# Eight orders of the products of a weight unit, taken in turn, with the order of all stream products fixed

## Chip, cores and metric

The kernel runs on one core of one Trainium2 chip. The metric is the device time of one execution in microseconds (us), lower is better. TensorE is called PE, VectorE DVE, ScalarE ACT; DMAs of the weights are issued from SyncE (SP).

## What is computed

The reference is a trunk of four residual layers on x of 256 tokens and 2048 channels: a state-space mixer, a gated conv feed-forward, a gated short convolution, and a second gated conv feed-forward, with a norm ahead of each and one at the end. Nearly all the work lies in products with large weight matrices. Cut to that:

```python
for i in range(DEPTH):                      # DEPTH = 2
    h = rms_norm(x, mix_norm_w[i])
    if i % 2 == 0:
        x = x + ssd_mixer(h, ...)           # u @ w_in (2048 x 10304), state-space part, y @ w_out (4096 x 2048)
    else:
        x = x + short_conv_mixer(h, ...)    # u @ w_in (2048 x 6144), conv, gate, @ w_out (2048 x 2048)
    h = rms_norm(x, ffn_norm_w[i])
    x = x + conv_ffn(h, ...)                # u @ w_up (2048 x 11264), conv, silu(g) * v, @ w_down (5632 x 2048)
return rms_norm(x, final_norm_w)
```

All values are float32.

## The kernel before

Every weight matrix is read once, in **units** of 256 rows (two slices k of 128 rows) by 512 columns (four column blocks t of 128). `load_unit` (lines 249 to 262) brings a unit in by a DMA from SP, ACT rounds it to a high part `wh` (line 260, the CAST), and DVE takes the rest as a low part `wl` (line 261). Four pairs of buffers `wh`, `wl` exist (`WB = 4`), so the cast of a unit waits until PE has used up the unit four places earlier. The activations lie in pairs of 128-channel slices, each split in a high and a low part that stand side by side in a tile `hl`.

`stream` (line 274) multiplies a run of units, mostly 8 of them, with the activations. For each of the eight (t, k) of a unit it issues a **wide** product, the high weights times high and low activations together, 512 columns (line 296), and a **narrow** one, the low weights times the high activations, 256 columns (line 297): 16 products. Where `one` is set (the streams for B, C and xs of the state-space mixer) the wide product is issued as two of 256 columns (lines 293 and 294), 24 products to a unit. All products of a (column block t) add up in one bank of PSUM; a stream has two tiles of two banks each, `pts[0]` for t = 0, 1 and `pts[1]` for t = 2, 3, out of a pool `psm` of three such tiles. So `pts[0]` of a stream takes the tile that is free, and `pts[1]` the tile that was `pts[0]` of the stream before, as soon as that has been read out. The reading out is done by `evac`: a copy by ACT (line 306) and a sum by DVE (line 308), or two sums by DVE (lines 634 and 636) in `residual_stream`, or one product with the norm's row (line 314) where `one` is set.

There are 84 streams of wide and narrow products with 696 units, 12 streams with `one` and 96 units, and the last down projection, in which tokens lie on partitions: 88 units of 12 products of 512 columns each (lines 794 to 796). Other matrix products (transposes, norm sums, the state-space part: lines 176, 183, 449, 566, 585, 593 and others) write to two further banks, `aux`.

The order in which PE takes its instructions is not that of the program text: the kernel is built with a scheduler that lays out each engine's queue by a model of the times. In the program's order a unit's products go t = 0, k = 0 wide, narrow; k = 1 wide, narrow; t = 1, and so on. The scheduler leaves this order in places. At the start of most streams it puts the products into `pts[0]` of the first units ahead of those into `pts[1]`, so that a narrow product of one tile is put off, or two wide ones follow each other; and at the end of the state-space mixer it interleaves products of two streams. There `ssd_gate` of the last group (line 603, under `tc.high_priority()`) prepares the last two pairs of activations of the first `residual_stream` of the output projection: its products with the six earlier units can run before that, those with the last two units cannot.

Of the kernel before, what the change touches and what calls it, by code (L numbers as in the profile page):

```python
# [13 lines left out]
PSUM = bass.MemoryType.PSUM  # L14
DRAM = bass.MemoryType.DRAM

P = 128
T = 256
# [14 lines left out]
KU = 2  # L33
COLS = 512
# [5 lines left out]
def trunk_kernel(ctx, tc, a, out):  # L40
    nc = tc.nc
    mm = nc.tensor.matmul
# [14 lines left out]
    psa = ctx.enter_context(tc.tile_pool(name="psa", bufs=2, space=PSUM))  # L57

    n_id = [0]

    def uid(s):
        n_id[0] += 1
# [5 lines left out]
    def aux():  # L68
        return psa.tile([P, 512], F32, tag="aux", name=uid("aux"))

# [1 line left out]
    mixer = ExitStack()  # L72
    bcpool = mixer.enter_context(tc.tile_pool(name="bcpool", bufs=4))
    xspool = mixer.enter_context(tc.tile_pool(name="xspool", bufs=3))
    start = ExitStack()
# [9 lines left out]
                in_=a["x"][0, c * P : (c + 1) * P, q * 512 : (q + 1) * 512],  # L85
            )

# [1 line left out]
    ident = cpool.tile([P, P], F32, tag="ident", name="ident")  # L89
    make_identity(nc, ident)  # L90
    ones = cpool.tile([P, P], F32, tag="ones", name="ones")
    nc.vector.memset(ones, 1.0)
    mask3 = cpool.tile([P, 3, P], F32, tag="mask3", name="mask3")
    # Nothing reads these products: they keep the tensor engine clocked up until x arrives.
    warm = psa.tile([P, 512], F32, tag="aux", name="warm")
    for _ in range(9):
        mm(warm[:, 0:P], ones, ones, start=True, stop=True)
# [3 lines left out]
    nc.vector.tensor_copy(mask3[:, 1, :], ones)  # L101
    nc.vector.tensor_copy(mask3[:, 2, :], triu)

# [1 line left out]
    rows = [  # L105
        ("mix", a["mix_norm_w"].rearrange("l (k p) -> (l k) p", p=P)),
        ("ffn", a["ffn_norm_w"].rearrange("l (k p) -> (l k) p", p=P)),
# [16 lines left out]
    for name, r in rows:  # L124
        base[name] = at
        lo = 0
        while lo < r.shape[0]:
            i, off = divmod(at, P)
# [20 lines left out]
    load_x(0)  # L149
    load_params(0)  # L150

# [1 line left out]
    def rsqrt(v, n):  # L153
        """v**-0.5 for v > 0, [P, n], from an integer seed by Newton's method."""
        r = small.tile([P, n], F32, tag="rs_r", name=uid("rs_r"))
        t = small.tile([P, n], F32, tag="rs_t", name=uid("rs_t"))
        sh = small.tile([P, n], I32, tag="rs_i", name=uid("rs_i"))
        ts(out=sh, in0=v.bitcast(I32), scalar1=1, scalar2=None, op0=ALU.logical_shift_right)
        ts(
            out=r.bitcast(I32), in0=sh, scalar1=-1.0, scalar2=float(0x5F3759DF),  # L160
            op0=ALU.mult, op1=ALU.add,
        )
        for _ in range(3):
            stt(out=t, in0=r, scalar=-0.5, in1=v, op0=ALU.mult, op1=ALU.mult)
            tt(out=t, in0=t, in1=r, op=ALU.mult)
            stt(out=r, in0=t, scalar=1.5, in1=r, op0=ALU.add, op1=ALU.mult)
        return r

    def bcast_tok(r):
        """r [tokens, 2] -> PSUM [P, 256], the same row on every partition."""  # L170
        dg = small.tile([P, 2, P], F32, tag="dg", name=uid("dg"))
        ps = aux()
        for c in range(2):
            ts(out=dg[:, c, :], in0=ident, scalar1=r[:, c : c + 1], scalar2=None, op0=ALU.mult)
        for c in range(2):
            mm(ps[:, c * P : (c + 1) * P], ones, dg[:, c, :], start=True, stop=True)  # L176
        return ps[:, :T]

    def tok_sum(acc):
        """Column sums of acc [P, 256] -> PSUM [tokens, 2]."""  # L180
        ps = aux()
        for c in range(2):
            mm(ps[:, c : c + 1], acc[:, c * P : (c + 1) * P], ones[:, 0:1], start=True, stop=True)
        return ps[:, 0:2]
# [11 lines left out]
        return (pool or hlpool).tile([P, 2, 2 * T], F32R, tag="hl", name=uid("hl"))  # L196

    def split_pair(hl, src, wname=None, k0=0):
        """hl[:, j] = [high | low] parts of src[:, j] (times a per-channel weight)."""
        if wname is None:  # L200
            nc.scalar.copy(hl[:, :, 0:T], src)
            tt(out=hl[:, :, T : 2 * T], in0=src, in1=hl[:, :, 0:T].bitcast(F32), op=ALU.subtract)
            return
        for j in range(2):
            w = pcol(wname, k0 + j)
            act(hl[:, j, 0:T], src[:, j, :], AF.Copy, scale=w)
            stt(  # L207
                out=hl[:, j, T : 2 * T], in0=src[:, j, :], scalar=w,
                in1=hl[:, j, 0:T].bitcast(F32), op0=ALU.mult, op1=ALU.subtract,
            )  # L210

# [1 line left out]
    s_in, s_out = a["ssd_w_in"][0], a["ssd_w_out"][0]  # L213
    c_in, c_out = a["sc_w_in"][0], a["sc_w_out"][0]
    plan = []
# [31 lines left out]
    units = []  # L247
# [14 lines left out]
        units.append((wh, wl))  # L262

    def weight_unit(c0, kc, ahead=WB - 1):
        """The next unit's [high], [low]; those that come after it are on their way."""
        i = taken[0]
        assert plan[i][1:] == (c0, kc), (plan[i], c0, kc)
        taken[0] += 1
        while len(units) < min(i + ahead + 1, len(plan)):
            load_unit()  # L270
        got, units[i] = units[i], None
        return got

    def stream(c0, hls, kcs, evac, one=False, before=None):
        """Products of COLS columns of w with the split activations; evac(pair, psum).

        The sum lies in columns 0..T of psum, or with one unset in two parts, 0..T and T..2T.
        """
        pts = [psm.tile([P, 2, 512], F32, tag="main", name=uid("main")) for _ in range(2)]
        n = len(kcs)  # L280
        for u in range(0, n, KU):
            if before is not None:
                before(u)
            wh, wl = weight_unit(c0, kcs[u], WB - 1 if before is None else 1)
            for t in range(4):
                o = pts[t // 2][:, t % 2, :]
                for k in range(KU):
                    i = u + k
                    hl = hls[i // 2][:, i % 2, :]
                    lw = slice(t * P, (t + 1) * P)  # L290
                    first, last = i == 0, i == n - 1
                    if one:
                        mm(o[:, 0:T], wh[:, k, lw], hl[:, 0:T], start=first, stop=False)  # L293
                        mm(o[:, 0:T], wh[:, k, lw], hl[:, T : 2 * T], start=False, stop=False)  # L294
                    else:
                        mm(o, wh[:, k, lw], hl, start=first, stop=False)  # L296
                    mm(o[:, 0:T], wl[:, k, lw], hl[:, 0:T], start=False, stop=last)  # L297
        if taken[0] < len(plan):
            while len(units) < min(taken[0] + WB - 1, len(plan)):
                load_unit()  # L300
        for p in range(2):
            evac(p, pts[p])
# [15 lines left out]
        return s  # L318

    def conv(s, width, wname, nk, k0, bname=None, tag="tp", pool=None):  # L320
        """Causal depthwise conv along tokens; channels k0*128.. of nk*128."""
        y = pair_tmp(tag, pool)
        for j in range(2):
            w = pcol(wname, (width - 1) * nk + k0 + j)
            if bname is None:
                act(y[:, j, :], s[:, j, :], AF.Copy, scale=w)
            else:
                act(y[:, j, :], s[:, j, :], AF.Identity, bias=pcol(bname, k0 + j), scale=w)  # L328
            for d in range(1, width):
                stt(  # L330
                    out=y[:, j, d:T], in0=s[:, j, 0 : T - d],
                    scalar=pcol(wname, (width - 1 - d) * nk + k0 + j),
                    in1=y[:, j, d:T], op0=ALU.mult, op1=ALU.add,
                )
        return y

    class Norm:
        """Sum of squares over channels, gathered pair by pair."""

        def __init__(self):  # L340
            self.acc = small.tile([P, 2, T], F32, tag="nacc", name=uid("nacc"), bufs=1)
# [17 lines left out]
            nc.scalar.copy(rb, ps)  # L359
            return rb  # L360

# [1 line left out]
    xp, xhl = [], []  # L363
    ss = small.tile([P, 2, 4], F32, tag="ss", name="ss")
    first = {}
# [37 lines left out]
    NCX = CONVD // P  # L403

    def bc_stream(g, o, before=None):
        """B (o = 0) or C (o = 1) of groups g..g+3."""
        res = []

        def evac(p, pt):
            k0 = DI // P + o * NG + g + 2 * p  # L410
            s = scaled(pt, first["r0"], True)
            y = conv(s, W_SSD, "ssdw", NCX, k0, "ssdb", "bc", bcpool)
            act(y, y, AF.Silu)
            res.append(y)

        stream(2 * DI + o * NG * DS + g * DS, xhl, range(NKD), evac, True, before)
        return res
# [1 line left out]
    bs = bc_stream(0, 0, x_pair)  # L419
    r_tok, r0 = first["r_tok"], first["r0"]  # L420

# [1 line left out]
    dtw = tokpool.tile([P, NKD, NH], F32, tag="dtw", name="dtw", bufs=1)  # L423
    nc.sync.dma_start(
        out=dtw, in_=s_in[:, DI + CONVD :].rearrange("(k p) h -> p k h", p=P)
# [73 lines left out]

    start.close()  # L500

# [1 line left out]
    sp = mixer.enter_context(tc.tile_pool(name="sp", bufs=2))  # L503
    decpool = mixer.enter_context(tc.tile_pool(name="decpool", bufs=3))

# [119 lines left out]
        return hls  # L625

    def residual_stream(hls, kcs, norm, nhl, nname, one=False):
        """x += products; when norm is given, x is final: gather its norm, split it."""
        for cg in range(D // COLS):

            def evac(p, pt, cg=cg):
# [36 lines left out]

    mixer.close()

# [1 line left out]
    NF = 2 * DFF // P  # L672
    gpool = ctx.enter_context(tc.tile_pool(name="gpool", bufs=3))
    hlpool2 = ctx.enter_context(tc.tile_pool(name="hlpool2", bufs=4))
# [33 lines left out]
            lambda m: ("mix", NKD + 2 * m),  # L708
        )

# [1 line left out]
    xhl, nhl = nhl, []  # L712
    r = norm.row()
    norm = Norm()
# [26 lines left out]
        yhl, range(NKD), norm, nhl, lambda m: ("ffn", NKD + 2 * m)  # L741
    )

# [1 line left out]
    xhl = nhl  # L745
    r = norm.row()
    tokpool = ctx.enter_context(tc.tile_pool(name="tokpool2", bufs=2))
# [28 lines left out]
    for part in range(2):  # L776
# [3 lines left out]
        for cg in range(D // COLS):  # L780
# [6 lines left out]
            def products(c, u):  # L787
                wh, wl = held[u]
                for k in range(KU):
# [1 line left out]
                    hl = hid[i // 2][:, i % 2, :]  # L791
                    hi_ = hl[:, c * P : (c + 1) * P]
                    lo_ = hl[:, T + c * P : T + (c + 1) * P]
                    mm(pt[:, c, :], hi_, wh[:, k, :], start=(i == 0), stop=False)  # L794
                    mm(pt[:, c, :], hi_, wl[:, k, :], start=False, stop=False)  # L795
                    mm(pt[:, c, :], lo_, wh[:, k, :], start=False, stop=(i == n - 1))  # L796

            def evac(c):
                x = xtok[c][:, cols]
# [49 lines left out]
```

## Time and profile before

| | |
|---|---|
| median of 2 runs | 2566.73 us (2564.36 to 2569.1) |
| the profiled execution | span 2563.7 us from its first to its last instruction; its own time outside the span isn't given |
| PE busy | 2545.1 us, 99% of the span |
| DVE, ACT busy | 1790.0 us (70%), 1311.8 us (51%) |
| granted PE clock | 0.998 on the mean |
| DMA | 478.76 MB, 187 GB/s |

A row of the timeline holds the start in us from the span's beginning, the duration, engine, source line, operation, the tile written, the tiles read, the shape, and how many instructions were merged (x1, x2); in brackets stands the idle time ahead and what ended it. The duration of a matmul overlaps that of the next, since they are pipelined, and its end is modelled: what a product costs is read from one start to the next start. A row of the windows gives, for one stretch, the busy time and the number of instructions that touch it, then the granted clock and the DMA share. Buffer numbers are left out of tile names.

### The profile page before, as it was taken

To read this page: it belongs to the slowest core of one execution; us is meant where nothing else is said; L and a number is where in the kernel's file an instruction comes from. 1 tells how busy PE (TensorE), PEld (TensorE's weight loads), DVE (VectorE), ACT (ScalarE), POOL (GpSimd) and SP (SyncE) were. 2 spreads that over 40 slices of the span, in tenths; PEclk is the share of its full clock that TensorE was granted. 3 is DMA by queue.
4 is the path that set the end of the run, shared out by engine and by line. 5 is a ranking of instruction groups with operands and counts; after the bars stand their busy time and mean duration, and the time that the engine had idled before them with its cause. 6 is when DMAs were issued, how large, how long until landed. Compare 5 with 4: busy or idle time off the path is not lost.

```text
span 2563.7 us, 38305 instructions
## 1 busy us (share of the span) xinstructions
PE 2545.1 (99%) x15101; PEld 2234.2 (87%) x15101; DVE 1790.0 (70%) x2600; ACT 1311.8 (51%) x1620; POOL 1.1 (0%) x8
## 2 busy tenths in 40 slices
PE   9999999999999999999999999999999999999998
PEld 8899998998888888888888888888888888888886
DVE  7788875788777776557776666666677764577764
ACT  5565543566555554345555444444555553455543
POOL 0000000000000000000000000000000000000000
PEclk9999999999999999999999999999999999999999
DMA  6666656665656555655555656566555566655564
GB/s 210 188 182 196 186 174 185 190 185 169 197 182 194 189 188 181 191 188 185 193 189 182 195 184 186 184 195 189 175 184 187 187 196 192 193 187 188 187 192 143
DMA packets 254696, 478.76 MB, mean 187 GB/s; under 512 B 17651, under 2 KB 27059, under 8 KB 254387
## 3 DMA queue, kind: packets, MB, share of 16 engines
q1 hardware_dynamic: 251856, 473.49, 59.0%
q10 hardware_dynamic: 2659, 2.82, 0.3%
q8 instruction: 118, 1.93, 0.3%
q14 instruction: 63, 0.52, 0.1%
HBM read 474.09 MB, written 2.16 MB: 186 GB/s over the span
## 4 chain that ended last, share of the span: by engine, by line
PE 97%; DMA 1%; DVE 1%; ACT 1%; issue 0%; SPq 0%; ACTq 0%; DVEq 0%
PE main L296 50%; PE main L297 28%; PE main L794 3%; PE main L796 3%; PE main L795 3%; PE main L293 3%; PE main L294 3%; DMA raw<-in_ssd_w_in_dram 1%; PE aux L585 1%; DMA cbc<-cs_d 0%; PE aux L449 0%; PE aux L593 0%; PE aux L566 0%; ACT wh L260 0%; DVE wl L261 0%; PE aux L176 0%
## 5 line engine op out<-in xcount | busy, mean ns | idle before, releaser
L296 PE MATMUL main<-hl,wh 128*128 128x512 f32 x5568 | 1944.3, 396 | 0.2 <-DVE hl L207 0.2
L297 PE MATMUL main<-hl,wl 128*128 128x256 f32 x6336 | 1749.9, 280 | 0.2 <-DVE wl L261 0.2
L261 DVE TENSOR_TENSOR wl<-raw,wh 128x1024 fp32r<-128x1024 f32 x880 | 1073.7, 1224 | 711.1 <-ACT wh L260 710.5
L260 ACT CAST wh<-raw 128x1024 fp32r<-128x1024 f32 x880 | 920.9, 1049 | 1080.6 <-PE main L296 734.4
L296 PEld LDWEIGHTS main<-hl,wh 128*128 128x128 f32 x5568 | 1035.2, 188 | 237.3 <-issue 1.6
L297 PEld LDWEIGHTS main<-hl,wl 128*128 128x128 f32 x6336 | 1196.3, 189 | 15.1 <-issue 1.1
L294 PE MATMUL main<-hl,wh 128*128 128x256 f32 x768 | 217.6, 284 | 0.0
L293 PE MATMUL main<-hl,wh 128*128 128x256 f32 x768 | 217.6, 286 | 0.0
L293 PEld LDWEIGHTS main<-hl,wh 128*128 128x128 f32 x768 | 146.9, 192 | 2.6 <-issue 2.2
L294 PEld LDWEIGHTS main<-hl,wh 128*128 128x128 f32 x768 | 147.4, 192 | 0.6 <-issue 0.6
L794 PE MATMUL main<-wh,hl 128*128 128x512 f32 x352 | 137.8, 392 | 0.8 <-DVE xtok L800 0.8
L796 PE MATMUL main<-wh,hl 128*128 128x512 f32 x352 | 137.7, 391 | 0.0
L795 PE MATMUL main<-wl,hl 128*128 128x512 f32 x352 | 137.6, 391 | 0.0
L330 DVE SCALAR_TENSOR_TENSOR tp<-tp,prm,tp 128x255 f32<-128x255 f32 x208 | 90.6, 477 | 0.0
L306 ACT COPY tp<-main 128x512 f32<-128x512 f32 x128 | 74.3, 581 | 28.9 <-PE main L297 28.9
L308 DVE TENSOR_TENSOR tp<-main,tp 128x512 f32<-128x512 f32 x128 | 87.6, 684 | 0.0
L794 PEld LDWEIGHTS main<-wh,hl 128*128 128x128 f32 x352 | 66.2, 188 | 15.5 <-DVE xtok L800 1.2
L796 PEld LDWEIGHTS main<-wh,hl 128*128 128x128 f32 x352 | 66.2, 188 | 14.5
L795 PEld LDWEIGHTS main<-wl,hl 128*128 128x128 f32 x352 | 66.2, 188 | 14.3
L330 DVE SCALAR_TENSOR_TENSOR g<-tp,prm,g 128x254 f32<-128x254 f32 (+1 forms) x176 | 74.7, 478 | 0.1
L328 ACT ACTIVATE g<-tp,prm,prm 128x256 f32<-128x256 f32 x88 | 48.2, 596 | 38.0 <-DVE tp L317 38.0
L317 DVE TENSOR_TENSOR tp<-tp,rrow 128x512 f32<-128x512 f32 x96 | 66.1, 689 | 1.8
(133 smaller groups left out, 957.8 us busy)
## 6 DMA issues: line engine op xcount, KB each, us to landing
raw<-in_ffn_w_up_dram SPq DMA_DIRECT2D x352, 512.0 KB, 4.1
raw<-in_ffn_w_down_dram SPq DMA_DIRECT2D x176, 512.0 KB, 3.6
raw<-in_ssd_w_in_dram SPq DMA_DIRECT2D x160, 512.0 KB, 4.6
raw<-in_sc_w_in_dram SPq DMA_DIRECT2D x96, 512.0 KB, 4.3
raw<-in_ssd_w_out_dram SPq DMA_DIRECT2D x64, 512.0 KB, 4.0
raw<-in_sc_w_out_dram SPq DMA_DIRECT2D x32, 512.0 KB, 4.3
cbc<-cs_d SPq DMA_DIRECT2D x32, 256.0 KB, 5.4
xt<-in_x_dram SPq DMA_DIRECT2D x8, 256.0 KB, 5.0
```

The costliest lines, as they stand in the source:

```text
L260: nc.scalar.copy(wh, raw)
L261: tt(out=wl, in0=raw, in1=wh.bitcast(F32), op=ALU.subtract)
L293: mm(o[:, 0:T], wh[:, k, lw], hl[:, 0:T], start=first, stop=False)
L294: mm(o[:, 0:T], wh[:, k, lw], hl[:, T : 2 * T], start=False, stop=False)
L296: mm(o, wh[:, k, lw], hl, start=first, stop=False)
L297: mm(o[:, 0:T], wl[:, k, lw], hl[:, 0:T], start=False, stop=last)
L306: nc.scalar.copy(pb, pt[:, :, T : 2 * T])
L308: tt(out=s, in0=pt[:, :, 0:T], in1=pb, op=ALU.add)
L330: stt(out=y[:, j, d:T], in0=s[:, j, 0 : T - d], scalar=pcol(wname, (width - 1 - d) * nk + k0 + j), in1=y[:, j, d:T], op0=ALU.mult, op1=ALU ...
L794: mm(pt[:, c, :], hi_, wh[:, k, :], start=(i == 0), stop=False)
L795: mm(pt[:, c, :], hi_, wl[:, k, :], start=False, stop=False)
L796: mm(pt[:, c, :], lo_, wh[:, k, :], start=False, stop=(i == n - 1))
```

## The change

The loops over t and k in `stream` are replaced by one loop over a list of (wide, t, k). The list comes from `unit_order(form)`, which has eight forms; the form is the number of the stream modulo 8, counted over streams without `one`. The first and the last unit of a stream, and all units of streams with `one`, keep form 0, the order of the program text before. Of 696 units with wide and narrow products 528 are neither first nor last: 64 to 68 for each form. In forms 0, 1, 2 and 5 four products in a row go to the same bank; in 3, 4, 6 and 7 two. Form 6 has all eight wide products of the unit first and then all eight narrow ones, form 5 has each narrow product ahead of its wide one.

Second, `follow` ties each stream product to the stream product issued before it (lines 293 to 297 and 794 to 796), by a dependence without a semaphore that holds for the order in the queue alone. So the scheduler must keep the products of all streams in the order of the program text; products into `aux` may still be put anywhere between them. `weight_unit`, the loads, the casts and `evac` are as they were. Comments are dropped.

```diff
+    last_main = [None]
+
+    def follow(inst):
+        if last_main[0] is not None:
+            tc.add_manual_dep(
+                inst.ins, last_main[0],
+                mybir.DependencyInfo(
+                    mybir.DependencyClass.NoSync, mybir.DependencyReason.DATA
+                ),
+                reason="stream order",
+            )
+        last_main[0] = inst.ins.name
...
+    turn = [0]
+
+    def unit_order(form):
+        ts_, ks = range(4), range(KU)
+        tk = [(t, k) for t in ts_ for k in ks]
+        if form == 0:
+            return [(w, t, k) for t, k in tk for w in (1, 0)]
+        if form == 1:
+            return [(w, t, k) for t in ts_ for w in (1, 0) for k in ks]
+        if form == 2:
+            return [(w, t, k) for n, (t, k) in enumerate(tk) for w in ((1, 0), (0, 1))[n % 2]]
+        if form == 3:
+            return [(w, 2 * h + t, k) for h in (0, 1) for w in (1, 0) for t in (0, 1) for k in ks]
+        if form == 4:
+            return [(w, t, k) for k in ks for t in ts_ for w in (1, 0)]
+        if form == 5:
+            return [(w, t, k) for t, k in tk for w in (0, 1)]
+        if form == 6:
+            return [(w, t, k) for w in (1, 0) for t, k in tk]
+        return [(w, 2 * h + t, k) for h in (0, 1) for k in ks for t in (0, 1) for w in (1, 0)]
...
-            for t in range(4):
+            edge = u == 0 or u == n - KU
+            for wide, t, k in unit_order(0 if one or edge else turn[0] % 8):
+                i = u + k
                 o = pts[t // 2][:, t % 2, :]
-                for k in range(KU):
-                    i = u + k
...
-                    if one:
-                        mm(o[:, 0:T], wh[:, k, lw], hl[:, 0:T], start=first, stop=False)
-                        mm(o[:, 0:T], wh[:, k, lw], hl[:, T : 2 * T], start=False, stop=False)
-                    else:
-                        mm(o, wh[:, k, lw], hl, start=first, stop=False)
-                    mm(o[:, 0:T], wl[:, k, lw], hl[:, 0:T], start=False, stop=last)
+                first = i == 0 and bool(wide)
+                last = i == n - 1 and not wide
+                if not wide:
+                    follow(mm(o[:, 0:T], wl[:, k, lw], hl[:, 0:T], start=False, stop=last))
+                elif one:
+                    follow(mm(o[:, 0:T], wh[:, k, lw], hl[:, 0:T], start=first, stop=False))
+                    follow(mm(o[:, 0:T], wh[:, k, lw], hl[:, T : 2 * T], start=False, stop=False))
+                else:
+                    follow(mm(o, wh[:, k, lw], hl, start=first, stop=False))
+        turn[0] += not one
...
-                    mm(pt[:, c, :], hi_, wh[:, k, :], start=(i == 0), stop=False)
-                    mm(pt[:, c, :], hi_, wl[:, k, :], start=False, stop=False)
-                    mm(pt[:, c, :], lo_, wh[:, k, :], start=False, stop=(i == n - 1))
+                    follow(mm(pt[:, c, :], hi_, wh[:, k, :], start=(i == 0), stop=False))
+                    follow(mm(pt[:, c, :], hi_, wl[:, k, :], start=False, stop=False))
+                    follow(mm(pt[:, c, :], lo_, wh[:, k, :], start=False, stop=(i == n - 1)))
```

More of the change, by code (lines that the diff above doesn't have):

```diff
@@ L284, in stream @@
             wh, wl = weight_unit(c0, kcs[u], WB - 1 if before is None else 1)
-            for t in range(4):
+            edge = u == 0 or u == n - KU
+            for wide, t, k in unit_order(0 if one or edge else turn[0] % 8):
+                i = u + k
                 o = pts[t // 2][:, t % 2, :]
-                for k in range(KU):
-                    i = u + k
-                    hl = hls[i // 2][:, i % 2, :]
-                    lw = slice(t * P, (t + 1) * P)
-                    first, last = i == 0, i == n - 1
-                    if one:
-                        mm(o[:, 0:T], wh[:, k, lw], hl[:, 0:T], start=first, stop=False)
-                        mm(o[:, 0:T], wh[:, k, lw], hl[:, T : 2 * T], start=False, stop=False)
-                    else:
-                        mm(o, wh[:, k, lw], hl, start=first, stop=False)
-                    mm(o[:, 0:T], wl[:, k, lw], hl[:, 0:T], start=False, stop=last)
+                hl = hls[i // 2][:, i % 2, :]
+                lw = slice(t * P, (t + 1) * P)
+                first = i == 0 and bool(wide)
[8 more added lines that the diff above has]
+        turn[0] += not one
         if taken[0] < len(plan):
```

## The prediction

> **What bounds the kernel now.** I read the page first, for the engine that has no idle time, then the waits, then windows of stretches that hold hardly anything but wide and narrow products, and last the timeline at stream starts.
>
> ```profile
> span 2563.7 us, 38305 instructions
> PE 2545.1 (99%) x15101; PEld 2234.2 (87%) x15101; DVE 1790.0 (70%) x2600; ACT 1311.8 (51%) x1620; POOL 1.1 (0%) x8
> PEclk9999999999999999999999999999999999999999
> L296 PE MATMUL main<-hl,wh 128*128 128x512 f32 x5568 | 1944.3, 396 | 0.2 <-DVE hl L207 0.2
> L297 PE MATMUL main<-hl,wl 128*128 128x256 f32 x6336 | 1749.9, 280 | 0.2 <-DVE wl L261 0.2
> ```
>
> PE is busy throughout at the full clock, and before its 5568 wide and 6336 narrow products it idled 0.4 us in all. So the time moves only by what a product costs from start to start, or by gaps that open on PE. The 2563.7 us are a span; the runs' median is 2566.73, 3.0 us more, which I add at the end.
>
> ```profile
> ACT wh L260 <- PE main L296: 734.4, 495, 6.2
> DVE wl L261 <- ACT wh L260: 710.5, 615, 3.8
> ```
>
> These are the longest waits. The casts wait for PE to give a weight buffer back, so the weights are ahead of PE and neither DMA nor ACT nor DVE sets the pace.
>
> ```profile
> 1130.00:1350.00 220.00, 220.00 (x1260) 191.87 (x1259) 159.85 (x212) 120.98 (x158) 0.00 (x0) 1.00 0.58 189
> 1470.00:1740.00 270.00, 270.00 (x1548) 235.47 (x1547) 170.81 (x194) 124.41 (x146) 0.00 (x0) 1.00 0.60 188
> ```
>
> Second and third column: PE busy and its matmuls. 220 us for 630 pairs is 349.2 ns for one wide and one narrow product; 270 for 774 is 348.8. I take 349 ns as a pair's price now.
>
> **What the order is worth to a pair.** The trace has two spacings for the same alternating order. Columns: start, duration, instruction; the first rows are the first and last of 44 wide products with a narrow one between each, the others of 39.
>
> ```profile
> 1484.69 0.39 PE L296 MATMUL main<-hl,wh 128*128 128x512 f32 x1
> ...
> 1499.59 0.40 PE L296 MATMUL main<-hl,wh 128*128 128x512 f32 x1
> ...
> 1508.68 0.40 PE L296 MATMUL main<-hl,wh 128*128 128x512 f32 x1
> ...
> 1522.11 0.40 PE L296 MATMUL main<-hl,wh 128*128 128x512 f32 x1
> ```
>
> 14.90 us over 43 pairs is 346.5 ns, 13.43 over 38 is 353.4. Neither has a wait in it, and I don't know what chooses between them. Now runs of one width alone. The last down projection has 512 columns only: 90 products between the first two rows, 42 between the next two. The streams with `one` have 256 columns only: 15 products between the last two.
>
> ```profile
> 2098.46 0.39 PE L794 MATMUL main<-wh,hl 128*128 128x512 f32 x1
> ...
> 2118.86 0.39 PE L794 MATMUL main<-wh,hl 128*128 128x512 f32 x1
> ...
> 2119.55 0.40 PE L794 MATMUL main<-wh,hl 128*128 128x512 f32 x1
> ...
> 2129.30 0.40 PE L794 MATMUL main<-wh,hl 128*128 128x512 f32 x1
> ```
>
> ```profile
> 77.88 0.28 PE L293 MATMUL main<-hl,wh 128*128 128x256 f32 x1
> ...
> 79.67 0.28 PE L293 MATMUL main<-hl,wh 128*128 128x256 f32 x1
> ```
>
> 20.40/90 = 226.7 ns, 9.75/42 = 232.1 ns, 1.79/15 = 119.3 ns. One wide and one narrow that never stand side by side thus cost 346.0 to 351.4 ns, alternating ones 346.5 to 353.4. The price belongs to a product's own width; what stands ahead of it doesn't show. A form that groups the widths (1, 2, 3, 6) is between these bounds too. Turns inside a stream and a change of bank can be seen where the scheduler left the program's order:
>
> ```profile
> 1278.44 0.28 PE L297 MATMUL main<-hl,wl 128*128 128x256 f32 x1
> 1278.56 0.62 PE L296 MATMUL main<-hl,wh 128*128 128x512 f32 x2
> 1279.02 0.28 PE L297 MATMUL main<-hl,wl 128*128 128x256 f32 x1
> ```
>
> Two wide products, the second into another bank, take 0.46 us from 1278.56 to 1279.02, 230 ns each. So no form has a price outside 346.0 to 353.4 ns in any row. **Term 1**: against 349 now, 5568 pairs give (346.0 - 349) x 5568 = -17 us to (353.4 - 349) x 5568 = +24 us if every pair took one spacing, the 168 edge units included, since both spacings occur in the old order as well. With no reason for either I take the middle of what the trace has, and set the term to 0.
>
> The weight loads stay one for each product and keep their cover. A form that needs all of `wl` early (5) or late (6) shifts the first or last use of a buffer by less than half a unit, 1.4 us, and the casts' wait of 734.4 us on PE is the spare time that takes it.
>
> **What the fixed order costs.** The scheduler's detours covered waits, and this cover goes. Four kinds of places:
>
> *Ordinary stream starts.* In the order of before, the stream that starts at 1275.09 sends its first product to `pts[1]` with the second wide one of the pair at 1278.56, 3.70 us later. In the program's order `pts[1]` is needed after eight products, four pairs, at 1275.09 + 1.39 = 1276.48. It is the tile that ACT and DVE read out last:
>
> ```profile
> 1275.09 0.39 PE L296 MATMUL main<-hl,wh 128*128 128x512 f32 x1
> ```
>
> ```profile
> 1273.91 0.59 ACT L306 COPY tp<-main 128x512 f32<-128x512 f32 x1 [0.41 <-PE main L297]
> ```
>
> ```profile
> 1274.67 0.68 DVE L308 TENSOR_TENSOR tp<-main,tp 128x512 f32<-128x512 f32 x1
> ```
>
> DVE is done at 1275.35, 1.13 us before the need. So the detour was not needed on the chip, and some 60 starts of this kind cost nothing; the evacuation hides under the last half unit of the old stream and the first half of the new.
>
> *Starts behind a residual stream.* There DVE reads twice (L634, L636):
>
> ```profile
> 1016.68 0.39 PE L296 MATMUL main<-hl,wh 128*128 128x512 f32 x1
> ```
>
> ```profile
> 1016.22 1.36 DVE L634 TENSOR_TENSOR x<-main,x 128x512 f32<-128x512 f32 x2
> 1017.49 1.28 DVE L636 TENSOR_TENSOR x<-main,x 128x512 f32<-128x512 f32 x2
> ```
>
> The row at 1017.49 holds two; the first ends near 1017.49 + 0.68 = 1018.17, the need is at 1016.68 + 1.39 = 1018.07. With a little for the signal that is 0.15 us, about 20 times: **+3 us**.
>
> *Starts in the state-space part, where DVE is behind.* The worst that I found:
>
> ```profile
> 122.67 0.28 PE L293 MATMUL main<-hl,wh 128*128 128x256 f32 x1
> ```
>
> ```profile
> 124.20 1.22 DVE L261 TENSOR_TENSOR wl<-raw,wh 128x1024 fp32r<-128x1024 f32 x1
> 125.33 0.69 DVE L308 TENSOR_TENSOR tp<-main,tp 128x512 f32<-128x512 f32 x1
> ```
>
> The need there comes after twelve products of 119.3 ns, at 124.10, the tile is free at 126.02: 1.9 us late. Five others are 0.5 to 0.9 late by the same reckoning. Together **+5.5 us**, unless the queues of ACT and DVE come out otherwise.
>
> *The gate of the last group.* The first residual stream of the output projection has used up what it may at 639.43, and the next stream was pulled ahead:
>
> ```profile
> 639.43 0.40 PE L296 MATMUL main<-hl,wh 128*128 128x512 f32 x1
> ...
> 641.08 0.61 PE L176 MATMUL aux<-dg,ones 128*128 128x128 f32 x4
> 641.88 0.39 PE L297 MATMUL main<-hl,wl 128*128 128x256 f32 x1 [0.19 <-DVE wl L261]
> ...
> 643.53 0.50 PE L296 MATMUL main<-hl,wh 128*128 128x512 f32 x1 [0.22 <-DVE hl L207]
> ```
>
> From 639.43 to 643.53 PE would be left with the four products of L176: 4.1 - 0.8 = **+3.3 us**. What is queued behind the waiting product is every later stream product, so the whole of it is lost. It could be less, since DVE would not need to split weights ahead of the gate's steps.
>
> **The sum.** 0 + 3 + 5.5 + 3.3 = 11.8 us on 2563.7 gives a span of 2575.5, and 3.0 us beside the span gives 2578.5 for the runs. That is +0.5%, and about 2% is what a measurement of this kernel can tell from no change. The gaps have bounds of 0 (the queues of DVE and ACT fall better) and some 25 us (each twice as long), the pairs of -17 and +24: 2550 to 2616.
>
> **Rivals.**
>
> *All pairs at the quick spacing.* If a fixed order settles the products in the first of the two spacings, term 1 is -14 to -17 us and eats the gaps: 2578.5 - 16 = 2562, and 2550 without the gaps. For it: long stretches hold it for 14.9 us. Against: the same order has held the other for 13.4 us. It stays within 2%. Chance 0.18.
>
> *Every stream start stalls (slower).* The scheduler's model saw a need to put `pts[1]` off to 3.70 us. With the order fixed it may lay the queues of ACT and DVE out otherwise, and put a cast (L260) and a split (L261) ahead of the evacuation. Place: the eight-product point of 84 streams. Price: from the split, 1.22 us, plus a cast of 1.05 (the row below), less the 1.13 us in hand: 1.1 us x 84 = 96 us, 2675. It decides over 2% from 51 us, 0.6 us a start. Against it: the evacuation begins 1.2 us ahead of the stream's start (1273.91), and the casts wait for PE anyway. Chance 0.07.
>
> ```profile
> 1275.18 1.05 ACT L260 CAST wh<-raw 128x1024 fp32r<-128x1024 f32 x1 [0.68 <-PE main L296]
> ```
>
> *Changing banks loosens PE and its clock drops.* Forms 3, 4, 6 and 7 turn to another bank after two products, not four: 262 units of 2.8 us (eight pairs). If PE paused at each turn and the granted clock fell by half there, these 734 us would grow by up to as much again; 7% of that is over 2%. The row at 1278.56 turns the bank without a pause, and PEclk stands at 9 in all slices. Chance 0.01. [...]
>
> *Grouping hides what lies between products.* Were wide products in a row cheaper than any seen, a gain of over 2% needs 51/5568 = 9 ns a pair, under 340. The rows of 90 wide products in a row say 226.7, so this has to come from something not shown. Chance 0.02.
>
> **How the numbers follow.** The forecast has 0.72, the quick spacing 0.18, both within 2%: 0.90. Slower than 2% gets 0.08, faster 0.02. The predicted time is that of the forecast, 2578 us; the range 2550 to 2615 takes in the bounds of both terms and leaves out the stalled starts.
>
> **What would show it.** Right: L296 and L297 with the durations of before, a windows row of 1130 to 1350 with 348 to 352 ns a pair, PE waits of 5 to 25 us in total, most on DVE readers of `main` at stream starts, on `hl` near 640 us and near 122 us; each form's streams of 16 k-slices as long as the others' to 2%. Wrong: a form whose units differ by over 2% from 2.8 us, PE waiting at ordinary feed-forward starts, or a granted clock below 9 in slices past the first.

## The result, and the profile after

The changed kernel takes 2579.1 us (median of 2 runs, 2578.66 to 2579.53), the one before 2566.73: ratio 1.0053, 95% interval 1.0036 to 1.0069. It is slower by half a percent. The forecast was 2578, the span 2575.5; the profiled span is 2577.7, 14.0 above that of before.

The page after, with the group rows of the wide (now L334) and narrow products (L329):

```profile
span 2577.7 us, 38335 instructions
PE 2552.1 (99%) x15101; PEld 2238.8 (87%) x15101; DVE 1787.9 (69%) x2600; ACT 1330.6 (52%) x1630; POOL 1.1 (0%) x8
L334 PE MATMUL main<-hl,wh 128*128 128x512 f32 x5568 | 1830.4, 397 | 4.2 <-DVE hl L220 1.8
L329 PE MATMUL main<-hl,wl 128*128 128x256 f32 x6336 | 1553.5, 281 | 0.0
```

The durations of one product, 397 and 281 ns, are those of before (396, 280). The busy column fell since products of one width now follow each other and the overlap of neighbours is counted to one row (the two wide products in the prediction's row at 1278.56 count 0.62 us, not twice 0.39); it says nothing of the time. What grew is the idle time in the last column, 0.2 to 4.2 us. PE idles 25.6 us in the span (2577.7 - 2552.1), 18.6 before. The waits of PE after:

```profile
PE aux L189 <- DVE dg L187: 3.2, 1, 3.2
...
PE main L334 <- DVE hl L220: 1.8, 1, 1.8
...
PE main L334 <- DVE tp L352: 1.5, 3, 0.7
...
PE main L331 <- DVE tp L346: 1.1, 1, 1.1
```

L189 and L220 are the steps of the gate, L352 and L346 the readers of `main` at stream starts. Two windows whose products are nearly all stream products (columns: window, its length, busy time and count of PE, PEld, DVE, ACT and POOL, granted clock, DMA share, GB/s):

```profile
1130.00:1350.00 220.00, 219.95 (x1255) 191.93 (x1256) 155.94 (x204) 119.48 (x150) 0.00 (x0) 1.00 0.64 189
...
1470.00:1740.00 270.00, 270.00 (x1547) 235.65 (x1546) 172.68 (x210) 125.64 (x147) 0.00 (x0) 1.00 0.63 187
```

A pair costs 220/627.5 = 350.6 and 270/773.5 = 349.1 ns, against 349.2 and 348.8 before. Over all wide and narrow products with a wide or narrow one on both sides, the mean start-to-start distances add up to 350.6 ns a pair, before 350.4, when distances that a wait draws out (over 300 ns behind a wide, 200 ns behind a narrow product) are left out.

**The eight forms.** These windows, PE's count alone, run from the start of the second unit of a stream to the start of the last: six middle units of forms 4, 5, 6, 7, 0, 1, 2, 3 in this order, 96 products each (the count takes in those that reach over the edges).

```profile
1604.43:1621.07 16.64, 16.64 (x99) 1.00 0.64 187
1626.61:1643.26 16.65, 16.65 (x98) 1.00 0.64 189
1648.90:1665.66 16.76, 16.76 (x98) 1.00 0.63 191
1671.31:1688.27 16.96, 16.96 (x98) 1.00 0.63 185
1693.93:1710.89 16.96, 16.96 (x98) 1.00 0.63 186
1716.54:1733.26 16.72, 16.72 (x98) 1.00 0.62 188
1738.91:1755.65 16.74, 16.74 (x98) 1.00 0.62 188
1761.59:1778.43 16.84, 16.84 (x99) 1.00 0.62 188
```

By unit that is 2773, 2775, 2793, 2827, 2827, 2787, 2790 and 2807 ns: all between the two spacings of before (346.5 x 8 = 2772 and 353.4 x 8 = 2827). The alternating forms take one end or the other, the grouped ones (6, 1, 2, 3) a value between. Form 4 has 2773 here and 2827 in other streams; form 1 has 2784 to 2787 in 61 of its 66 middle units.

**The gate.** PE after, from the end of what it may do of the first residual stream:

```profile
640.15 0.28 PE L329 MATMUL main<-hl,wl 128*128 128x256 f32 x1
643.62 0.68 PE L189 MATMUL aux<-dg,ones 128*128 128x128 f32 x4 [3.19 <-DVE dg L187]
646.14 0.79 PE L334 MATMUL main<-hl,wh 128*128 128x512 f32 x1 [1.84 <-DVE hl L220]
...
646.95 0.63 PE L334 MATMUL main<-hl,wh 128*128 128x512 f32 x1
...
647.59 0.63 PE L334 MATMUL main<-hl,wh 128*128 128x512 f32 x1
...
652.02 0.40 PE L334 MATMUL main<-hl,wh 128*128 128x512 f32 x1
```

Two gaps, 3.2 and 1.8 us; then the products come 640 ns a pair apart (646.95 to 647.59) until 652.02, not 350. The windows of PE there, with the granted clock behind the count:

```profile
640.20:646.20 6.00, 0.97 (x7) 0.91 0.55 175
646.20:651.90 5.70, 5.70 (x18) 0.50 0.53 184
652.00:657.70 5.70, 5.63 (x33) 1.00 0.31 92
```

The second of these stretches in the kernel before:

```profile
646.20:651.90 5.70, 5.70 (x33) 1.00 0.71 253
```

After the gaps the clock stands at 0.50 through the second stretch, and 18 products touch it where 33 did in the kernel before. The mean of 0.91 ahead of it holds another 1.1 us of half clock, so it lasts about 6.8 us. It sets in before the second gap is over: the clock is 1.00 up to 645.0 and 0.50 from 645.2 on. Ahead of that lie the gap of 3.2 us, 0.7 us of small products and 0.8 us of the second gap, which is 1.8 us long in all; which of them it takes wasn't shown.

### The profile page after: what moved, and what is told of

Same layout as the page of the kernel before. It is cut to its first block, busy times and chain, and to the rows that moved or that the text cites. A ratio compares the mean times of both kernels' runs of the same rounds, so it can differ in the third digit from the quotient of the medians.

```text
span 2577.7 us, 38335 instructions
## 1 busy us (share of the span) xinstructions
PE 2552.1 (99%) x15101; PEld 2238.8 (87%) x15101; DVE 1787.9 (69%) x2600; ACT 1330.6 (52%) x1630; POOL 1.1 (0%) x8
## 4 chain that ended last, share of the span: by engine, by line
PE 96%; DVE 2%; DMA 2%; ACT 1%; issue 0%; SPq 0%; ACTq 0%; DVEq 0%
PE main L334 50%; PE main L329 28%; PE main L832 3%; PE main L834 3%; PE main L833 3%; PE main L331 3%; PE main L332 3%; DMA raw<-in_ssd_w_in_dram 1%; PE aux L623 1%; DVE wl L274 0%; DMA cbc<-cs_d 0%; PE aux L487 0%; PE aux L604 0%; PE aux L631 0%; ACT wh L273 0%
## 5 line engine op out<-in xcount | busy, mean ns | idle before, releaser
L334 PE MATMUL main<-hl,wh 128*128 128x512 f32 x5568 | 1830.4, 397 | 4.2 <-DVE hl L220 1.8
L329 PE MATMUL main<-hl,wl 128*128 128x256 f32 x6336 | 1553.5, 281 | 0.0
L329 PEld LDWEIGHTS main<-hl,wl 128*128 128x128 f32 x6336 | 1152.8, 189 | 66.2 <-issue 1.4
L334 PEld LDWEIGHTS main<-hl,wh 128*128 128x128 f32 x5568 | 994.7, 188 | 192.9 <-issue 6.1
L331 PEld LDWEIGHTS main<-hl,wh 128*128 128x128 f32 x768 | 147.5, 192 | 2.5 <-DVE tp L346 1.3
L332 PEld LDWEIGHTS main<-hl,wh 128*128 128x128 f32 x768 | 147.7, 192 | 0.3 <-issue 0.3
L346 DVE TENSOR_TENSOR tp<-main,tp 128x512 f32<-128x512 f32 x128 | 87.6, 685 | 6.9 <-ACT tp L344 6.9
```

The costliest lines, as they stand in the source:

```text
L329: follow(mm(o[:, 0:T], wl[:, k, lw], hl[:, 0:T], start=False, stop=last))
L331: follow(mm(o[:, 0:T], wh[:, k, lw], hl[:, 0:T], start=first, stop=False))
L332: follow(mm(o[:, 0:T], wh[:, k, lw], hl[:, T : 2 * T], start=False, stop=False))
L334: follow(mm(o, wh[:, k, lw], hl, start=first, stop=False))
L346: tt(out=s, in0=pt[:, :, 0:T], in1=pb, op=ALU.add)
```

## The experiments

All are compared with the kernel before, run on the same chip in the same session. Spacings of units are distances of the starts in the trace.

**Old order, fixed.** Form 0 everywhere.

```diff
-            for wide, t, k in unit_order(0 if one or edge else turn[0] % 8):
+            for wide, t, k in unit_order(0):
```

> Every unit in form 0, the order of all stream products fixed as in the changed kernel. Theory A, the 14 us come from gaps that the fixed order opens (about 7.5 at the gate near 650 us, 4 at the starts behind residual streams, the rest at starts in the state-space part) and the eight forms add up to nothing: the gaps are all here, so 2565 to 2595 by the spacing that the alternating order happens to hold (2773 or 2827 ns a unit: 696 units are 1930 or 1967 us), with the gaps visible on PE. Rival B, the forms cost it: as before, about 2567, no gap near 650 us. With one order throughout, the units from 680 to 1800 us should all show one and the same spacing, 2773 or 2827, since only two wide or two narrow products in a row were seen to change it.

2584.1 us, ratio 1.0071 (1.0056 to 1.0086). The slowdown is there without any new order of products. PE's count in two stretches of that run:

```profile
742.00:990.00 248.00, 248.00 (x1405) 1.00 0.63 186
1127.00:1349.00 222.00, 221.93 (x1281) 1.00 0.63 190
```

353.0 ns a pair in the first and 346.6 in the second, and so from end to end: eleven streams hold the one spacing, ten the other. It is 2827 ns up to the residual streams near 1000 us, 2773 behind them and 2827 from 1487 to 1757; so not one and the same from 680 to 1800 as expected. It changed where PE had waited at a residual start, where a product into `aux` came between, and at 1349 us, in the first units of a down projection, with neither. 463 of its 696 units fall near 2827 and 143 near 2773.

Read at the same products as in the kernel before, this run loses 4.9 us at the gate, from 593 to 673 us, and not 7.5, and 12.9 us from there to the last down projection, where the change loses 5.7. Its 14 starts behind residual streams with a wait of 0.3 us make 4 us of the 12.9; the rest is left for the slow spacing, which the old order in its fixed place holds for long and the eight forms in turn don't. So the slowdown comes back without a new order, but about half of it is not gaps; what the forms themselves cost is settled by the next run.

**Eight forms, order free.**

```diff
     def follow(inst):
-        if last_main[0] is not None:
+        if False:
```

> The eight forms, but no dependence between stream products: the scheduler may move them as before. Theory A: the gaps are gone, 2563 to 2570, ratio to the kernel before 0.998 to 1.002, PE idle near 650 us under 1 us. Rival B: 2577 to 2581 as with the change.

2565.2 us, ratio 0.9999 (0.9990 to 1.0009): nothing is left of the slowdown, though all forms are there. The window at the gate, all engines (PE's busy time and count first):

```profile
600.00:690.00 90.00, 89.50 (x529) 76.64 (x528) 68.64 (x104) 46.85 (x61) 0.00 (x0) 1.00 0.59 188
```

The clock is 1.00 and PE lacks 0.5 us of 90; with the change it lacked 5.2. So the fixed order costs the time, not the forms: theory A.

**The gate free.** As the change, with `follow` switched off during the residual streams behind the last gate.

```diff
     def follow(inst):
+        if free[0]:
+            last_main[0] = None
+            return
...
+    free[0] = True
     residual_stream(yhl, range(16, 32), norm, nhl, lambda m: ("ffn", 2 * m))
+    free[0] = False
```

> The changed kernel with the order left free in one place: the four residual streams of the output projection behind the last gate. Theory A: the 7.5 us between 595 and 677 us come back, 2570 to 2573, no stretch of half clock near 650 us. Rival, the gate is late for another reason than the order (the queues of DVE): 2577 to 2580.

2574.4 us, ratio 1.0033 (1.0022 to 1.0045): some 5 us come back of the 7.5 expected, a partial miss.

```profile
646.58 0.50 PE L338 MATMUL main<-hl,wh 128*128 128x512 f32 x1 [1.84 <-DVE hl L224]
```

```profile
600.00:690.00 90.00, 87.23 (x515) 74.73 (x514) 68.37 (x106) 47.80 (x61) 0.00 (x0) 1.00 0.56 178
```

The half clock is gone and so is the wait of 3.2 us, which the pulled-ahead products fill. The wait for `hl` stays, at 646.58, 3.1 us later than before: the steps of the gate themselves run late, and the free order doesn't heal that. From 595 us to the end of the second residual stream this run loses 2.1 us on the kernel before, the change 7.5.

**The starts free.** As the change, but `follow` leaves out the first three units of each stream (`follow` itself as in the run before).

```diff
             edge = u == 0 or u == n - KU
+            free[0] = u < 3 * KU
```

> The eight forms as in the changed kernel, but the first three units of each stream are left out of the fixed order, so that the scheduler can put off their products into the second PSUM tile and pull the next stream ahead at the gate; five of eight units stay fixed. Theory A: the gaps lie at the starts and at the gate alone, so nearly all 14 us come back: 2563 to 2570, stall sum near that of before. Rival, the fixed order in the body of a stream costs too: 2572 to 2580.

2564.2 us, ratio 0.9999 (0.9990 to 1.0009). Everything comes back with five of eight units still fixed. From 690 to 1830 us no wide or narrow product follows another over 0.1 us late in this trace, while with the change ten do, and from 600 to 690 us PE waits 0.5 us in all. The cost lies at the starts of streams and at the gate, which this edit frees too, and on balance none of it in the body of a stream.

**Form 1 in all middle units**, order fixed.

```diff
-            for wide, t, k in unit_order(0 if one or edge else turn[0] % 8):
+            for wide, t, k in unit_order(0 if one or edge else 1):
```

> Form 1 (two wide, two narrow) in all middle units, order fixed. Theory C, a grouped form has a spacing of its own (form 1: 2787 ns a unit) while the mean of the eight is 2803: 528 units x 16 ns = 8.5 us less, 2568 to 2573. Rival D, the spacing is only inherited from what ran before, whatever the form: as with the change, 2576 to 2582.

2569.7 us, ratio 1.0015 (1.0006 to 1.0025), some 9 us under the change, where theory C (a grouped form keeps its own spacing, form 1 2787 ns a unit) expected 8.5.

**Form 1 in all units, order free.**

```diff
-        if last_main[0] is not None:
+        if False:
...
-            for wide, t, k in unit_order(0 if one or edge else turn[0] % 8):
+            for wide, t, k in unit_order(0 if one else 1):
```

> Form 1 in all 696 units, order free. Theory A and C: no gaps, and a unit of 2787 ns against some 2800 now in the kernel before: 696 x 13 = 9 us less than before, 2555 to 2560. Rival: the scheduler breaks the groups up and the old mixture is back: 2564 to 2568.

2555.0 us (4 runs, 2554.16 to 2555.71), ratio 0.9957 (0.9942 to 0.9971): the fastest version of the study, faster than both kernels. Three stretches of feed-forward and short conv, first of this run, then the same stretches of the kernel before:

```profile
742.00:990.00 248.00, 248.00 (x1425) 1.00 0.59 189
1135.00:1336.00 201.00, 201.00 (x1156) 1.00 0.59 189
1471.00:1740.00 269.00, 269.00 (x1546) 1.00 0.61 189
```

```profile
742.00:990.00 248.00, 248.00 (x1422) 1.00 0.58 188
1135.00:1336.00 201.00, 201.00 (x1151) 1.00 0.58 188
1471.00:1740.00 269.00, 269.00 (x1542) 1.00 0.60 188
```

3 to 5 products more in each, 0.2 to 0.4%. The scheduler's detours at stream starts don't disturb it: from 935 to 1671 us most units are 2786 or 2787 ns, the first ones of the down projections 2776 to 2817.

**Form 2 in all units but the last, order free.**

```diff
-        if last_main[0] is not None:
+        if False:
...
-            for wide, t, k in unit_order(0 if one or edge else turn[0] % 8):
+            for wide, t, k in unit_order(0 if one or u == n - KU else 2):
```

> Form 2 (wide, narrow, narrow, wide) in all units but the last of a stream, order free. Theory C, a grouped form has a spacing of its own and form 2 had 2787 ns a unit like form 1: 2554 to 2559, as with form 1. Rival, what is won is peculiar to form 1: 2563 to 2568.

2562.9 us, ratio 0.9992 (0.9982 to 1.0002), between the two expectations. Most units in the body are 2786 to 2794 as expected, but the last units, in form 0, come to 2814 and the first units of the next streams to about 2809. What the body wins these two mostly give back.

**Narrow ahead of wide (form 5) in all but first units**, order fixed, and then fixed only within a stream and free at the gate.

```diff
-            edge = u == 0 or u == n - KU
-            for wide, t, k in unit_order(0 if one or edge else turn[0] % 8):
+            form = 0 if one or u == 0 else 5
+            for wide, t, k in unit_order(form):
...
```

Left out is the flag that closes a sum, which now stands on a wide product. The second run adds to this:

```diff
+        last_main[0] = None
...
+    free[0] = True
     residual_stream(yhl, range(16, 32), norm, nhl, lambda m: ("ffn", 2 * m))
+    free[0] = False
```

The first added line stands at the start of each stream, the others as in the run with the gate free.

> Form 5 (narrow ahead of wide) in every unit but the first of a stream, order fixed. In the changed kernel the middle units of form 5 came out at 2773 ns nearly everywhere, whichever spacing ran before. Theory C, an order that starts with two narrow products in a row sets the quick spacing: 612 units near 2773, 84 first units slower, against 2803 on the mean of the eight forms: 18 to 20 us less than with the change, 2556 to 2564. Rival D, chance: 2573 to 2585.

> As the run before, but the order fixed only within a stream, and free in the four residual streams behind the last gate. Theory A and C: besides the quick spacing, the gaps at the gate (7.5 us) and behind residual streams (4 us) come back: 2545 to 2556, faster than the kernel before by 0.4 to 0.8%. Rival: the scheduler's changes at the stream ends put the slow spacing back: 2560 to 2570.

2577.1 us, ratio 1.0045 (1.0028 to 1.0062), and 2569.2, ratio 1.0013 (1.0004 to 1.0022): theory C missed in both, and both results lie in the rival's range. Four streams of the first, from the third unit of each to its end (six units):

```profile
747.24:763.88 16.64, 16.64 (x98) 1.00 0.59 189
769.51:786.47 16.96, 16.96 (x97) 1.00 0.60 186
792.03:808.67 16.64, 16.64 (x97) 1.00 0.59 189
814.31:831.27 16.96, 16.96 (x98) 1.00 0.59 186
```

The spacing goes to and fro, stream by stream. Two narrow products in a row don't set the quick one. In the second run the order inside a stream kept the waits at the starts, 13 of 0.3 us from 712 us on, so those gaps stayed: from 712 us, where it was 1.9 us ahead of the kernel before, it falls 3.4 us behind at the end.

**One swap a stream.** Form 0 fixed; in the second unit the first four products go wide, wide, narrow, narrow. One run.

```diff
+        if form == 8:
+            w8 = [(w, t, k) for t, k in tk for w in (1, 0)]
+            return [w8[0], w8[2], w8[1], w8[3]] + w8[4:]
...
+            for wide, t, k in unit_order(8 if u == KU and not one else 0):
```

> All units in form 0, order fixed, as in the run with the old order fixed, but in the second unit of each stream the first four products go wide, wide, narrow, narrow. Theory E, only two alike in a row (or a product into aux, or a stall) change the spacing: between 742 and 991 us, and between 1127 and 1349, where that run held one spacing, the units from the second on differ from the first in at least some streams, and never change later in the stream. Rival, the spacing depends on something else that runs in time: the same pattern as in that run. Time 2563 to 2590 either way.

2584.05 us. Six units of each of three streams, from the third unit to the stream's end:

```profile
1131.88:1148.52 16.64, 16.64 (x99) 1.00 0.61 192
1154.11:1171.07 16.96, 16.96 (x99) 1.00 0.58 186
1176.71:1193.67 16.96, 16.96 (x98) 1.00 0.59 186
```

The second stream begins at the quick spacing (first unit 2774 ns) and leaves the swap at the slow one; between 1127 and 1349 the run without swaps was quick all through. So a swap can change the spacing, within an otherwise even stretch, as theory E said. But it did so in this one stream of the two stretches: from 742 to 991 us all come in slow and stay slow, and the first stream above has the same swap and stays quick. Further on, at 1878 us, one comes in slow (2819 ns) and leaves the swap quick (2773).

## Why the prediction was right

The time and the mechanism held, and two of the terms were mis-sized in opposite directions. That 2578 came so near to 2579.1 is luck in part: the state-space starts were put 4.6 us too high and the gate 4.2 too low, and the 3.0 us added beside the span are 1.8 in the run of the profile (2579.53 less 2577.7), while the forecast of the span, 2575.5, was 2.2 short. The forecast also held about 2% for the least that a measurement can tell from no change; the interval of 1.0036 to 1.0069 tells half a percent. Delays against before are read at the same product in both traces.

- **Term 1, the pairs: 0, bounds -17 to +24.** Measured +0.2 ns a pair, 1 us. The reading that no form lies outside what the old order already had was right, and form for form too, though the alternating order has a third value between the two that it named (last section). Right as a sum only because eight forms average out: one form throughout gave 9 us less (form 1), form 0 throughout 5 us more.
- **Ordinary starts: nothing.** Right. After most feed-forward and short-conv streams the next stream's first unit has 2773 to 2831 ns, so PE did not wait at the eighth product.
- **Starts behind residual streams: +3 us, 20 times 0.15.** Measured 13 times 0.3, 4 us; at four starts there is no wait, and at three products into `aux` stand in its place. The wait is there, at the product foretold:

```profile
1028.17 0.28 PE L329 MATMUL main<-hl,wl 128*128 128x256 f32 x1
1028.53 0.47 PE L334 MATMUL main<-hl,wh 128*128 128x512 f32 x1
1028.83 0.28 PE L329 MATMUL main<-hl,wl 128*128 128x256 f32 x1
```

0.36 us from narrow to wide where 0.12 is the rule, and 0.07 more behind it.

- **Starts in the state-space part: +5.5 us.** Four were found late, 3.7 us together; the worst waited where it was foretold, by 1.4 us and not 1.9:

```profile
126.13 0.38 PE L329 MATMUL main<-hl,wl 128*128 128x256 f32 x1
127.61 0.38 PE L331 MATMUL main<-hl,wh 128*128 128x256 f32 x1 [1.10 <-DVE tp L346]
```

But by 594 us the kernel was only 0.9 us behind: other places in that part got quicker by nearly as much, which the forecast had no term for. I haven't traced these one by one.

- **The gate: +3.3 us.** This step failed in its size: 7.5 us between 595 us (delay 0.9) and the end of the second residual stream at 677 us (8.4). The forecast took the moment at which `hl` was ready in the old trace, 643.53. It came at 646.14, since the chain that leads there was late well ahead of the gate's last steps. The last `decay` product and the second product with `z`, first in the kernel before, then with the change:

```profile
621.97 0.96 DVE L554 TENSOR_TENSOR decay<-decay,cb 128x768 f32<-128x768 f32 x1 [1.47 <-ACT decay L552]
...
628.08 0.69 DVE L610 TENSOR_TENSOR yg<-yg,z 128x512 f32<-128x512 f32 x1
```

```profile
624.36 0.96 DVE L592 TENSOR_TENSOR decay<-decay,cb 128x768 f32<-128x768 f32 x1
...
631.54 0.69 DVE L648 TENSOR_TENSOR yg<-yg,z 128x512 f32<-128x512 f32 x1
```

The chain is 2.4 us late at the first and 3.5 at the second; from there to `hl` it catches up 0.9. Splits of weights among the later steps are not the reason: behind the second row four stand in DVE's queue with the change, six before. The queues of the engines came out otherwise; why is open.

And the forecast left out what the two gaps did to the clock: nine pairs at 640 instead of 353 ns are 2.6 us more. Idle 5.0 us, less the 0.4 that PE idled here before, half clock 2.6 and one start of 0.3 behind a residual stream make the 7.5 us.

Sum: two of the 13 starts, at 445 and 654 us, lie inside the first two figures, so it is 0.9 + 7.5 + 11 x 0.3 + 1 = 12.7 of 14.0 us; 1.3 us isn't placed. Forecast 11.8.

Of the rivals, stalls at every start did not come about. Changes of bank after two products cost nothing: form 6, which has them, runs at 2793 ns a unit, at clock 1.00. Groups cheaper than any row of before were not seen. A quick spacing throughout, forecast at 14 to 17 us, was not reached in any run; form 1 in all units with the order free, 10.5 us under the kernel before, came nearest.

## What to carry to other kernels

Before costing a new order of matmuls, look for the same neighbours in the old trace, wherever a scheduler, another loop or an odd tile has put them: here their start-to-start distances bounded the change on both sides. With eight forms in turn, the order fixed by hand cost time where the scheduler's detours had covered a wait, at the seams between streams and in front of a serial chain, and not in the body; so free the seams and fix the body, if at all, and look at what spacing a fixed body settles into. Cost a gap on PE with what follows it: here 5.0 us of idling brought 2.6 us more at half clock.

## What the runs showed of the hardware

The same alternating order of 512- and 256-column products runs at 346.6 or at 353.3 ns a pair, and in the run with the old order fixed kept what it had for ten and eleven streams, 222 and 248 us. In the first four or five units of the down projections it has a value between, 2801 to 2823 ns a unit in the run with the old order fixed (the streams from 990 and 1349 us), about 351 ns a pair; the kernel before has it near 1346 us too. The activations of the first four units lie in a pool of their own there (`hlpool2`); that this is the cause wasn't tried. Changes of the spacing were seen around two products of one width in a row, a product into `aux`, a wait, and these first units; after a swap it came out either way (in the run with one swap 2774 to 2827 ns a unit at 1154 us, 2819 to 2773 at 1878). Products grouped by width have a value of their own (348.3 ns a pair for two wide, two narrow) in nearly all units where no product into `aux` stands between. What sets the spacing of the alternating order is open: two narrow in a row and a single swap were tried, and neither gave a rule. Whether it hangs on the phase in which a weight load (0.19 us in the trace) meets the product ahead was not tried.
